# A hybrid decoder layer whose order is made by a cost model: new figures in the model, and a 64-row block transposed by VectorE instead of TensorE

## The chip, the cores and the metric

The kernel runs on one core of a Trainium2 chip. The metric is the time of one execution on the device in microseconds (us); lower is better. A core has five engines that run side by side, each with its own queue that it works through in order: TensorE (PE; its weight loads are listed apart as PEld), VectorE (DVE), ScalarE (ACT), GpSimd (POOL) and SyncE (SP), which issues most of the DMAs. An engine waits for another one on semaphores.

## The reference: what is computed

One decoder layer on 2048 tokens of width 1024, in float32. A mixer of two parallel head groups and an MLP, each followed by a layer norm:

```python
o = chunk_gated_delta_rule(q, k, v, g, beta)      # 8 heads of 128, chunks of tokens
m = memory_attention(mq, mem_k, mem_v)            # 4 heads over 256 memory rows
mix = concatenate([rms_norm(o) * silu(z), m]) @ w_out
x = layer_norm(ALPHA * x + mix)
x = layer_norm(ALPHA * x + square(relu(x @ w1)) @ w2)
```

The projection of x gives q, k, v (each through a causal convolution of four taps and a SiLU), the gate z, the decay and beta, and the memory query. Inside a chunk the delta rule solves a triangular system. The kernel does it with chunks of 128 tokens, by inverting a unit lower triangular matrix:

```python
lower = where(strict, (k_beta @ k.T) * decay, 0.0)
a_mat = eye + lower
u = triangular_solve(a_mat, v_beta, lower=True, unit_diagonal=True)
```

## The kernel before

**Tiling.** The tokens go in four blocks of 512 (`NB` blocks of `TB`). Each block passes three stages: the DeltaNet stage (projections, convolution, inversion, state scan, memory attention), the output projection with the first norm, and the MLP with the second. The MLP's second matrix product is done in seven products of sums of quarter matrices instead of eight (`ff_seven`, a Strassen-like scheme listed in `SEVEN`, L987); the sums of weight quarters are made in block 0 by `keep_sums` and put into a DRAM scratch called `tsc`, from which all blocks read them.

**Precision.** A large product is made of three fp32r matmuls, high x high, high x low and low x high (`mm3`). So each weight tile is loaded into `wraw` (three buffers), split by ACT (the high part) and DVE (the low part) into `whl` (four buffers), and read by PE. Tiles named `aq`, `ak`, `av`, `az`, `amq`, `ao`, `af` are PSUM results of such products, 24 matmuls of 512 columns each for a projection.

**DeltaNet by heads.** In step t of a block, `dense` projects head t, `gdn_a` prepares head t-1 (its matrix `dl`, the inversion, `ptv`), and `gdn_b` runs the state scan of head t-2 over four chunks of 128 tokens: pc and po on PE, R on DVE, vt on ACT, state on DVE. All are recorded one after the other but overlap in time.

**The inversion** (`invert`, L732). Four 128x128 matrices of a head are inverted together. 16-row blocks are solved on DVE in 15 steps (tiles `Xc` and `Bc`). Then the blocks are merged three times, to 32, 64 and 128 rows. Each merge has a product `pq` on PE, a copy to `Q` on ACT, a product `pp` on PE, and a subtraction or a multiply by -1 on DVE. `Y3` holds the transposed inverse; `X32` and `X64` hold the untransposed blocks that `pp` needs as weights. For the last merge, `X64` is made from `Y3` by four 64x64 transposes on PE into `px` (L799 to L801) and a copy by DVE (L802). Tiles pq, px and pp of one head parity share one PSUM bank (`ga0` or `ga1`).

**What sets the order.** The program isn't issued as it is written. `Recorder` (L135) keeps every operation, `cost` (L184) gives it a duration, and `issue` (L220) runs a list schedule: at each step the engine that is free first takes, of its operations that are ready, the one that was recorded first. The order so found is then issued to the engines' queues. All of these instructions therefore carry the line L320 in the profile, and are told apart by their tiles' names. For PE the model has two figures per matmul: `load` for the weights, which may overlap the matmul before, and `last` for the streaming. An operation that another engine releases counts as ready after a latency (`LAT`, `LAT_FROM`, L33 and L34) and a margin of 30 ns (`MARGIN`). A DMA takes 1700 ns and its bytes at a modelled rate, one after the other.

**Memory.** `raw` (two buffers in pool `tp`) holds a projection before the convolution; `keep_sums` uses it too. Behind `tp` lies a pool `pad` with one tile of 112 words that nothing reads (L372, L373), and behind that the pools `sp` and `sm`.

Of the kernel before, what the change touches and what calls it, by code (L numbers as in the profile page):

```python
# [8 lines left out]
F32 = mybir.dt.float32  # L9
# [5 lines left out]
P = 128  # L15
TB = 512
NC = TB // P
# [17 lines left out]
MARGIN = 30  # L35


def _prod(v):
    r = 1
    for a in v:  # L40
        r *= a
    return r
# [92 lines left out]
class Recorder:  # L135
# [47 lines left out]
    @staticmethod  # L183
    def cost(o, name, wr, rd, args, kw):  # L184
        e = o.eng
        shapes = [r.shape for r in wr] + [r.shape for r in rd]
        n = max([_prod(s[1:]) for s in shapes] or [1])
        if e == "PE":
            rhs = kw.get("rhs", args[2])
            mo, n = _prod(args[1].shape[1:]), _prod(rhs.shape[1:])  # L190
            f32 = name == "transpose" or isinstance(rhs, Ref) and rhs.buf.dtype == F32
            o.load = 0.8 * mo
            o.last = 2.4 + (0.8334 if f32 else 0.4167) * n
            if name == "transpose":
                return o.last
            if f32:
                return o.last + max(o.last, o.load)
            return o.last
        psum = any(r.buf.psum for r in rd + wr)
        if e == "SP":  # L200
            o.extra = 1700 + _prod(wr[0].shape if wr else rd[0].shape) * 4 / 250.0
            return 450
        scal = [v for v in args[2:] if isinstance(v, Ref)] if name.startswith("tensor_scalar") else []
        scal += [v for k, v in kw.items() if k in ("scalar", "scalar1", "scale", "bias") and not isinstance(v, (int, float))]
        if e == "ACT":
            n = _prod((wr[0]).shape[1:])
            return 52 + 0.833 * n + (0 if psum else 42) + 93 * len(scal) + ((305 if scal else 198) if "accum_out" in kw else 0)
        if e == "DVE":
            fast = not psum and name in ("tensor_copy", "tensor_scalar_mul", "tensor_scalar_add", "tensor_scalar_max",
                                         "memset")  # L210
            return 68 + (0.52 if fast else 1.042) * n + 62 * len(scal) + (7 * n if name == "reciprocal" else 0)
        if name == "memset":
            return 40 + 0.83 * n
        if kw.get("op") == ALU.pow:
            return 300 + 165 * n
        if name == "tensor_copy":
            return 119 + 3.34 * n
        return 150 + 2.1 * n if name == "tensor_tensor" else 176 + 3.34 * n

    def issue(self):  # L220
# [49 lines left out]
        while True:  # L270
            while pending:
                place(pending.pop(0))
            best = None
            for e in engs:
                if avail[e]:
                    t = free[e]
                elif soon[e]:
                    t = max(free[e], soon[e][0][0])
                else:
                    continue  # L280
                if best is None or t < best[0]:
                    best = (t, e)
            if best is None:
                break
            t, e = best
            while soon[e] and soon[e][0][0] <= t:
                r, i, o = heapq.heappop(soon[e])
                heapq.heappush(avail[e], (o.prio, i, o))
            o = heapq.heappop(avail[e])[2]
            if e == "PE":  # L290
                t = max(t, fed + o.load)
                fed = t + o.dur - o.last
            o.start, o.end = t, t + o.dur
            free[e] = o.end
            if o.extra:
                dma[0] = max(o.end + 1700, dma[0]) + o.extra - 1700
                o.end = dma[0]
            out.append(o)
            for s in o.succ:
                lat = LAT.get((e, s.eng), LAT_FROM[e])  # L300
                if lat:
                    lat += MARGIN
                s.ready = max(s.ready, o.end + lat)
                s.npred -= 1
                if s.npred == 0:
                    pending.append(s)
            for b in o.bufs:
                b.users -= 1
                b.end = max(b.end, o.end)
                if b.users == 0:  # L310
                    heapq.heappush(slots[b.key], b.end + LAT_FROM[e] + MARGIN)
                    again(b.key)
# [24 lines left out]
def hybrid_layer(  # L337
# [24 lines left out]
    nc = tc.nc  # L362
# [6 lines left out]
    cst = ctx.enter_context(tc.tile_pool(name="cst", bufs=1))  # L369
    wp = ctx.enter_context(tc.tile_pool(name="wp", bufs=1))  # L370
    tp = ctx.enter_context(tc.tile_pool(name="tp", bufs=1))
    pad = ctx.enter_context(tc.tile_pool(name="pad", bufs=1))  # L372
    nc.vector.memset(pad.tile([P, 112], F32, name="shift"), 0.0)  # L373
    sp = ctx.enter_context(tc.tile_pool(name="sp", bufs=1))
    sm = ctx.enter_context(tc.tile_pool(name="sm", bufs=1))
    ps = ctx.enter_context(tc.tile_pool(name="ps", bufs=1, space=bass.MemoryType.PSUM))
# [296 lines left out]
    def dense(b, h, T, G, w0=None):  # L673
        res = {}
        for nm, o in (("q", QO), ("k", KO), ("v", VO), ("z", ZO)):
            w = w0 if w0 and nm == "q" else load_in(b, o // P + h)
            a = bank("a" + nm, "acc")
            project(a, w, T)
            c = slot("c" + nm, "d")
            th = slot("th", "th")  # L680
            if nm == "z":
                nc.scalar.activation(th, a, AF.Tanh, scale=0.5)
                nc.vector.scalar_tensor_tensor(out=c, in0=th, scalar=1.0, in1=a, op0=ALU.add, op1=ALU.mult)
            else:
                gi = o // P + h
                raw = rec.buf(tp, (P, TB + 3), F32, "raw", 2, "raw")
                nc.scalar.copy(out=raw[:, 3:], in_=a)
                nc.gpsimd.tensor_copy(raw[:, 0:3], halo[:, gi].part(gi))
                if b < NB - 1:
                    nc.gpsimd.tensor_copy(halo[:, gi].part(gi), raw[:, TB:TB + 3])  # L690
                nc.scalar.activation(c, a, AF.Copy, scale=cw[:, 72 + gi:73 + gi])
                for j in range(3):
                    nc.vector.scalar_tensor_tensor(out=c, in0=raw[:, j:j + TB], scalar=cw[:, j * 24 + gi:j * 24 + gi + 1],
                                                   in1=c, op0=ALU.mult, op1=ALU.add)
                nc.scalar.activation(th, c, AF.Tanh, scale=0.5)
                nc.vector.scalar_tensor_tensor(out=c, in0=th, scalar=1.0, in1=c, op0=ALU.add, op1=ALU.mult)
            res[nm] = c
            if nm in "qk":
                if "kq" not in res:
                    res["kq"] = [rec.buf(tp, (P, 2, TB), F32R, "kq%d" % u, 1, "kq") for u in range(2)]  # L700
                i = "kq".index(nm)
                split(c, res["kq"][0][:, i].part(i), res["kq"][1][:, i].part(i), KQE)
# [29 lines left out]
    def invert(L, par):  # L732
# [47 lines left out]
        nc.vector.transpose(Z.rearrange("p c f -> p (c f)"), ZT.rearrange("p c f -> p (c f)"))  # L780
        for p in range(2):
            nc.vector.tensor_copy(X32[32 * p:32 * p + 32, :, 32 * p:32 * p + 32], Z[64 * p:64 * p + 32])
        for r in quads:
            nc.scalar.copy(out=Y3[r, :, r], in_=ZT[r])
        pq = bank("pq", "ga%d" % par)[:64, :P].rearrange("p (c f) -> p c f", c=NC)
        for c in range(NC):
            nc.tensor.matmul(pq[:, c], L32[:, c], ZT[:, c], start=True, stop=True)
        nc.scalar.copy(out=Q[:64, :, :32], in_=pq)
        pp = bank("pp", "ga%d" % par)[:64, :P].rearrange("p (c f) -> p c f", c=NC)
        for c in range(NC):  # L790
            nc.tensor.matmul(pp[:, c], X32[:, c], Q[:, c, :32], start=True, stop=True)
        for p in range(2):
            nc.vector.tensor_scalar_mul(Y3[64 * p:64 * p + 32, :, 64 * p + 32:64 * p + 64],
                                        pp[32 * p:32 * p + 32], -1.0)

        pq = bank("pq", "ga%d" % par)[:64, :2 * P].rearrange("p (c f) -> p c f", c=NC)
        for c in range(NC):
            nc.tensor.matmul(pq[:, c], L[:, c, :64], Y3[:, c, 64:], start=True, stop=True)
        px = bank("px", "ga%d" % par)[:64, :2 * P].rearrange("p (c f) -> p c f", c=NC)  # L799
        for c in range(NC):  # L800
            nc.tensor.transpose(px[:, c], Y3[:64, c, :64], ident[:64, :64])  # L801
        nc.vector.tensor_copy(X64[:64], px)  # L802
        nc.scalar.copy(out=Q[:64], in_=pq)
        pp = bank("pp", "ga%d" % par)[:64, :2 * P].rearrange("p (c f) -> p c f", c=NC)
        for c in range(NC):
# [165 lines left out]
    def keep_sums(u, j):  # L971

        if j == 0:
            B = [t[:, n * TB:(n + 1) * TB].part(n) for t in (tok_tile("wq"), tok_tile("wq")) for n in range(2)]
        else:
            B = [rec.buf(tp, (P, TB + 3), F32, "raw", 2, "wq")[:, :TB] for _ in range(2)]
            kq = rec.buf(tp, (P, 2, TB), F32, "kq1", 1, "wq")
            B += [kq[:, n].part(n) for n in range(2)]
        for n in range(4):
# [11 lines left out]
    def ff_seven(b, ff1_tiles, relu2, add, norm2):  # L991
        Q = 2 * P
        for g in range(NS):
# [45 lines left out]
            if last:  # L1039
                gb = load_bcast(ln2_g, "l2g"), load_bcast(ln2_b, "l2b")  # L1040
            banks = {}
            for n, (xn, wn, bn, on, (th, nh)) in enumerate(SEVEN):
                if not on:
                    banks[bn] = [bank("af2", ("ga%d" % t) if bn == "A" else "pb") for t in range(2)]
                w = [None, None]
# [223 lines left out]
```

## Time and profile before

| what | us |
|---|---|
| median of three runs | 2998.03 |
| lowest and highest of them | 2996.6 and 2998.27 |
| the profiled execution | 2999.08 |
| its span, from the first to the last instruction | 2997.4 |

A block of 512 tokens takes some 734 us. The stages of the second block are the pattern for the third and the fourth: DeltaNet from 784 to 1108 us after the span's start, output projection to 1184, MLP to 1518. Block 0 has its DeltaNet stage from 0 to 350, with the memory's keys and values and the high and low parts of the input weights made beside it.

How to read the rows. A row of the timeline has the start, the duration, engine, line, operation, out<-in, the shape, a count of merged instructions and, in brackets, the idle time of the engine before it and what ended that. A group row has busy time and the mean in ns of one instruction, then idle time before the group. For a matmul, "64*64" is the size of the weight block. Matmuls are pipelined, so a matmul's own duration is longer than the distance from its start to the next one's start; the distance is what one matmul costs. An instruction that waits holds up all behind it in its engine's queue.

### The profile page before, as it was taken

The page shows a single profiled execution, that of the slowest core. Times are in us where ns is not written, and L with a number is a line of the kernel's source. Part 1 is how long each engine was busy: PE and PEld are TensorE (multiplying, and loading weights), DVE is VectorE, ACT ScalarE, POOL GpSimd, SP SyncE. Part 2 cuts the span into 40 slices and gives each one's busy share as a digit, 9 for nine tenths or more (in the row PEclk, how much of TensorE's full clock was granted, in tenths as well). Part 3 has the DMA queues.
Part 4 walks back from the last instruction along what each step waited for, and adds up shares of the span by engine and source line. Part 5 has one row for each costly group of instructions (what it writes and reads, how often), then busy time and mean ns, then how long its engine had stood idle before and what let it go on. Part 6 is the DMA issues. An engine that isn't in the chain of part 4 may idle for free.

```text
span 2997.4 us, 43880 instructions
## 1 busy us (share of the span) xinstructions
PE 2945.4 (98%) x15300; PEld 2428.1 (81%) x15300; DVE 2168.6 (72%) x5537; ACT 1520.3 (51%) x3582; POOL 332.4 (11%) x808
## 2 busy tenths in 40 slices
PE   7999999999999999999999999999999999999998
PEld 6888788888788878888878887888878888788886
DVE  6898977666777787655577887665667787675667
ACT  5676534544355562544445665344554556444443
POOL 1222100000112211000012221000001222000000
PEclk9999999999999999999999999999999999999999
DMA  6765566656733223444473332244446332324443
GB/s 231 253 218 180 196 209 224 200 183 192 268 142 132 106 89 102 145 137 133 151 268 130 121 119 92 87 152 144 145 159 250 126 134 96 99 88 146 143 147 134
DMA packets 127709, 469.85 MB, mean 157 GB/s; under 512 B 14464, under 2 KB 16896, under 8 KB 109056
## 3 DMA queue, kind: packets, MB, share of 16 engines
q1 hardware_dynamic: 126912, 467.00, 46.2%
q8 instruction: 120, 1.97, 0.3%
q14 instruction: 101, 0.83, 0.1%
q10 hardware_dynamic: 576, 0.06, 0.0%
HBM read 402.97 MB, written 64.03 MB: 156 GB/s over the span
## 4 chain that ended last, share of the span: by engine, by line
PE 88%; DVE 8%; ACT 2%; issue 1%; DMA 1%; POOL 0%; POOLq 0%; ACTq 0%; DVEq 0%; SPq 0%
PE af L320 42%; PE ao L320 8%; PE aq L320 6%; PE ak L320 5%; PE az L320 5%; PE av L320 4%; PE amq L320 3%; PE pc L320 3%; PE pp L320 2%; PE pq L320 2%; PE po L320 2%; PE pkq L320 1%; DVE y L320 1%; PE sps L320 1%; DVE ck L320 1%
## 5 line engine op out<-in xcount | busy, mean ns | idle before, releaser
L320 DVE TENSOR_TENSOR whl<-wraw,whl 128x1024 fp32r<-128x1024 f32 (+1 forms) x446 | 538.7, 1216 | 392.8 <-ACT whl L320 386.1
L320 PE MATMUL af<-Thi,whl 128*128 128x512 f32 (+1 forms) x2304 | 655.9, 369 | 6.9 <-DVE whl L320 4.0
L320 ACT CAST whl<-wraw 128x1024 fp32r<-128x1024 f32 (+1 forms) x446 | 466.1, 1045 | 381.8 <-PE af L320 169.0
L320 PEld LDWEIGHTS af<-Thi,whl 128*128 128x128 f32 x2304 | 421.7, 191 | 78.5 <-DVE whl L320 4.8
L320 PE MATMUL af<-whl,xh 128*128 128x512 f32 x1536 | 476.4, 391 | 3.6 <-DVE whl L320 3.6
L320 PE MATMUL af<-Tlo,whl 128*128 128x512 f32 (+1 forms) x1152 | 424.8, 369 | 0.0
L320 PE MATMUL af<-whl,xl 128*128 128x512 f32 x896 | 347.3, 390 | 0.0
L320 PEld LDWEIGHTS af<-whl,xh 128*128 128x128 f32 x1536 | 288.6, 188 | 68.6 <-DVE whl L320 6.7
L320 PE MATMUL ao<-whl,ch 128*128 128x512 f32 x768 | 249.4, 399 | 0.5 <-DVE y L320 0.5
L320 PEld LDWEIGHTS af<-Tlo,whl 128*128 128x128 f32 x1152 | 220.4, 191 | 34.8
L320 ACT ACTIVATE rl<-af 128x512 f32<-128x512 f32 x128 | 76.5, 598 | 271.0 <-PE af L320 269.0
L320 DVE SCALAR_TENSOR_TENSOR y<-y,af 128x512 f32<-128x512 f32 x224 | 151.3, 684 | 84.1 <-PE af L320 82.9
L320 PEld LDWEIGHTS af<-whl,xl 128*128 128x128 f32 x896 | 168.5, 188 | 35.5
L320 POOL TENSOR_SCALAR ve<-mv 128x1 f32<-128x1 f32 x34 | 23.3, 684 | 1528.8 <-DVE mv L320 1528.8
L320 PE MATMUL aq<-Thi,whl 128*128 128x512 f32 x512 | 181.6, 414 | 7.5 <-ACT Thi L320 7.5
L320 PE MATMUL av<-Thi,whl 128*128 128x512 f32 x512 | 173.0, 402 | 0.0
L320 PE MATMUL ak<-Thi,whl 128*128 128x512 f32 x512 | 172.9, 401 | 0.0
L320 PE MATMUL az<-Thi,whl 128*128 128x512 f32 x512 | 170.2, 400 | 0.0
L320 PEld LDWEIGHTS ao<-whl,ch 128*128 128x128 f32 x768 | 142.6, 188 | 27.0 <-DVE y L320 0.7
L320 PE MATMUL ao<-whl,cl 128*128 128x512 f32 x384 | 153.5, 400 | 0.0
L320 PEld LDWEIGHTS aq<-Thi,whl 128*128 128x128 f32 x512 | 94.3, 192 | 21.5 <-ACT Thi L320 7.5
L320 PEld LDWEIGHTS az<-Thi,whl 128*128 128x128 f32 x512 | 95.9, 190 | 18.8 <-DVE whl L320 0.5
(252 smaller groups left out, 5756.3 us busy)
## 6 DMA issues: line engine op xcount, KB each, us to landing
wraw<-in_w_ff_dram SPq DMA_DIRECT2D x224, 512.0 KB, 4.0
whl<-wsc SPq DMA_DIRECT2D x108, 1024.0 KB, 4.8
wraw<-tsc SPq DMA_DIRECT2D x128, 512.0 KB, 3.3
wsc<-whl SPq DMA_DIRECT2D x36, 1024.0 KB, 4.9
wraw<-in_w_out_dram SPq DMA_DIRECT2D x48, 512.0 KB, 4.1
wraw<-in_w_in_dram SPq DMA_DIRECT2D x35, 512.0 KB, 5.8
wq<-in_w_ff_dram SPq DMA_DIRECT2D x64, 256.0 KB, 4.3
tsc<-wq SPq DMA_DIRECT2D x64, 256.0 KB, 3.3
```

The lines of the kernel that those rows point to most:

```text
L320: o.fn(*[res(a) for a in o.args], **{k: res(v) for k, v in o.kw.items()})
```

## The change

Four things change in the planner's model: a weight load is modelled as 4 + 0.84 ns per column instead of 0.8 ns per column; an fp32r matmul streams for 13.4 + 0.4167 ns per column instead of 2.4 + 0.4167; a DMA runs at 300 GB/s instead of 250; and an operation on PE that another engine releases counts as ready a weight load later. In the inversion, the four transposes to `px` and their copy go. `X64` is put together from parts: its two diagonal 32-row blocks are copied by POOL from `Z`, and the block below the diagonal comes from a VectorE transpose of the 32-row product `pp`, in PSUM, into a free part of `Lq`, and a multiply by -1. In the first group of block 0, product `A12` is recorded as the second of the seven instead of the sixth. The `pad` pool goes and each of the two `raw` buffers grows by 56 words.

```diff
-            o.load = 0.8 * mo
-            o.last = 2.4 + (0.8334 if f32 else 0.4167) * n
+            o.load = 4 + 0.84 * mo
+            o.last = 2.4 + 0.8334 * n if f32 else 13.4 + 0.4167 * n
...
-            o.extra = 1700 + _prod(wr[0].shape if wr else rd[0].shape) * 4 / 250.0
+            o.extra = 1700 + _prod(wr[0].shape if wr else rd[0].shape) * 4 / 300.0
...
-                    lat += MARGIN
+                    lat += MARGIN + (s.load if s.eng == "PE" else 0)
...
-    pad = ctx.enter_context(tc.tile_pool(name="pad", bufs=1))
-    nc.vector.memset(pad.tile([P, 112], F32, name="shift"), 0.0)
...
-                raw = rec.buf(tp, (P, TB + 3), F32, "raw", 2, "raw")
-                nc.scalar.copy(out=raw[:, 3:], in_=a)
+                raw = rec.buf(tp, (P, TB + 3 + 56), F32, "raw", 2, "raw")
+                nc.scalar.copy(out=raw[:, 3:TB + 3], in_=a)
...
             nc.vector.tensor_copy(X32[32 * p:32 * p + 32, :, 32 * p:32 * p + 32], Z[64 * p:64 * p + 32])
+            nc.gpsimd.tensor_copy(X64[32 * p:32 * p + 32, :, 32 * p:32 * p + 32], Z[32 * p:32 * p + 32])
...
-        pp = bank("pp", "ga%d" % par)[:64, :P].rearrange("p (c f) -> p c f", c=NC)
+        p32 = bank("pp", "ga%d" % par)
+        pp = p32[:64, :P].rearrange("p (c f) -> p c f", c=NC)
         for c in range(NC):
             nc.tensor.matmul(pp[:, c], X32[:, c], Q[:, c, :32], start=True, stop=True)
+        t32 = Lq[:32].rearrange("p f c -> p (f c)")
+        nc.vector.transpose(t32, p32[:32, :P])
         for p in range(2):
             nc.vector.tensor_scalar_mul(Y3[64 * p:64 * p + 32, :, 64 * p + 32:64 * p + 64],
                                         pp[32 * p:32 * p + 32], -1.0)
+        nc.vector.tensor_scalar_mul(X64[32:64, :, :32], t32.rearrange("p (c f) -> p c f", c=NC), -1.0)
...
-        px = bank("px", "ga%d" % par)[:64, :2 * P].rearrange("p (c f) -> p c f", c=NC)
-        for c in range(NC):
-            nc.tensor.transpose(px[:, c], Y3[:64, c, :64], ident[:64, :64])
-        nc.vector.tensor_copy(X64[:64], px)
...
-            B = [rec.buf(tp, (P, TB + 3), F32, "raw", 2, "wq")[:, :TB] for _ in range(2)]
+            B = [rec.buf(tp, (P, TB + 3 + 56), F32, "raw", 2, "wq")[:, :TB] for _ in range(2)]
...
-            for n, (xn, wn, bn, on, (th, nh)) in enumerate(SEVEN):
+            order = [0, 5, 1, 2, 3, 4, 6] if b == 0 and g == 0 else range(7)
+            for n, (xn, wn, bn, on, (th, nh)) in enumerate(SEVEN[i] for i in order):
```

## The prediction

> **What bounds the kernel now.** I read the page first: engine shares, clock, chain.
>
> ```profile
> span 2997.4 us, 43880 instructions
> ...
> PE 2945.4 (98%) x15300; PEld 2428.1 (81%) x15300; DVE 2168.6 (72%) x5537; ACT 1520.3 (51%) x3582; POOL 332.4 (11%) x808
> ...
> PE 88%; DVE 8%; ACT 2%; issue 1%; DMA 1%; POOL 0%; POOLq 0%; ACTq 0%; DVEq 0%; SPq 0%
> ```
>
> TensorE (PE) is busy 98% of the span, and 88% of the chain that ended last is its own instructions. Only 2997.4 - 2945.4 = 52 us are idle. Where they lie is shown by the busy time per stage; the columns are PE, weight loads, DVE, ACT, POOL, then the granted clock (near 1 throughout), the DMA share and GB/s.
>
> ```profile
> 0.00:80.00 80.00, 64.18 (x317) 51.46 (x318) 55.70 (x115) 43.79 (x99) 15.43 (x49) 0.96 0.69 240
> 80.00:350.00 270.00, 269.67 (x1594) 221.56 (x1593) 242.07 (x860) 177.36 (x535) 65.26 (x162) 1.00 0.60 210
> 784.00:1108.00 324.00, 320.31 (x1859) 262.32 (x1857) 255.80 (x964) 181.20 (x602) 67.95 (x185) 1.00 0.40 143
> 1184.00:1518.00 334.00, 331.72 (x1548) 276.36 (x1547) 210.01 (x302) 162.10 (x225) 5.15 (x7) 0.99 0.47 149
> 2652.00:2997.00 345.00, 332.08 (x1551) 278.36 (x1549) 219.16 (x314) 157.42 (x217) 7.38 (x11) 0.98 0.43 139
> ```
>
> The start leaves PE idle for 15.8 us and the last stage, with the closing layer norms, for 12.9. A DeltaNet stage (784 to 1108, and its two repeats) leaves 3.7, an MLP stage 2.3. So about 52 - 28.7 = 23 us of idle time lie where a better order could fill them. The rest must come from PE doing less. A PE that counts as busy may still stand behind a weight load or a change of shape, so I then looked at starts in the timeline rather than at busy time.
>
> **The change, part by part. The transposes.** Each of the 32 inversions sends four 64x64 transposes (px) to PE. The first fence is the chain's price of dense and of 128x128 fp32 work, the second the timeline around one px group.
>
> ```profile
> 832.01 5.45 PE az L320 x24
> ...
> 842.71 0.44 PE ptq L320 x4
> ```
>
> ```profile
> 943.31 0.37 ACT L320 COPY Q<-pq 64x256 f32<-64x256 f32 x1 [2.86 <-PE pq L320]
> ...
> 943.72 0.39 PE L320 MATMUL aq<-Thi,whl 128*128 128x512 f32 x1
> 944.03 0.25 PEld L320 LDWEIGHTS px<-ident,Y 64*64 64x64 f32 x4 [0.36 <-ACT Q L320]
> 944.04 0.41 PE L320 MATMUL px<-ident,Y 64*64 64x64 f32 x4
> ...
> 944.38 0.19 PEld L320 LDWEIGHTS ak<-Thi,whl 128*128 128x128 f32 x1
> 944.38 0.50 PE L320 MATMUL ak<-Thi,whl 128*128 128x512 f32 x1
> ...
> 944.71 0.39 PE L320 MATMUL ak<-Tlo,whl 128*128 128x512 f32 x1
> ```
>
> A dense matmul takes 5.45 / 24 = 0.227 us. From the aq matmul at 943.72 to the second ak at 944.71 are 0.99 us; without px they would hold two dense matmuls, 0.45. One group therefore costs 0.54 us, not the 0.34 from 944.04 to 944.38: PE loses about 0.09 before px and 0.11 after it, where ak's first weights load at the same moment as the matmul is shown to start. The profile puts the first loss on ACT's copy of Q, but that copy ended at 943.68, 0.35 us before the load: not a late operand. If it were, pp, which needs the same Q, would inherit 32 x 0.09 = 2.9 us. I take it to go.
>
> The Trainium skill, in "TensorEngine Tiling (Array Packing)", section Tiling Modes (Key Properties), says that "Changing tiling mode (not just tile) drains the TensorE"; a 64x64 block between 128x128 ones changes it twice. By that rule both losses go with px; by the profile's own releaser the sum is 2.9 us smaller. The trace agrees with the rule: the stop stands there with Q long done.
>
> 32 x 0.54 = 17.3 us. Six groups are split, two in each of the last three token blocks; the first and the last:
>
> ```profile
> 891.32 0.36 PE L320 MATMUL px<-ident,Y 64*64 64x64 f32 x3
> 891.61 0.49 PE L320 MATMUL pc<-vt,kd 128*128 128x128 f32 x2
> 891.93 0.39 PE L320 MATMUL po<-vt,at 128*128 128x128 f32 x2
> 892.25 0.24 PE L320 MATMUL px<-ident,Y 64*64 64x64 f32 x1
> 892.42 0.73 PE L320 MATMUL av<-Thi,whl 128*128 128x512 f32 x2
> ```
>
> ```profile
> 2432.35 0.36 PE L320 MATMUL px<-ident,Y 64*64 64x64 f32 x3
> ...
> 2433.27 0.24 PE L320 MATMUL px<-ident,Y 64*64 64x64 f32 x1
> ```
>
> Of the 1.10 us from 891.32 to 892.42, pc and po need about 0.44 (four at 0.44 / 4 = 0.11, as the ptq row has it); with 0.09 before and 0.11 after, px costs 0.86, 0.32 more than an unsplit group. 6 x 0.32 = 1.9, together **19.2 us of PE**. A second of PE is a second of span only where PE carries the chain, 88% by the page: 16.9 us. Bounds: nothing (rival C) to 19.2.
>
> **What replaces them.** On DVE one copy X<-px goes, a transpose of 32x128 from PSUM and a multiply into X64 come; on POOL two copies.
>
> ```profile
> L320 DVE TENSOR_SCALAR Y<-pp 32x128 f32<-32x128 f32 x64 | 18.0, 281 | 9.8 <-PE pp L320 8.7
> ...
> L320 DVE COPY X<-Z 32x128 f32<-32x128 f32 x64 | 14.2, 221 | 0.9
> L320 DVE COPY X<-px 64x256 f32<-64x256 f32 x32 | 13.3, 416 | 14.8 <-PE px L320 14.4
> ...
> L320 DVE STREAM_TRANSPOSE ZT<-Z 128x128 f32<-128x128 f32 x32 | 9.9, 309 | 0.4
> ```
>
> ```profile
> L320 POOL COPY L<-dl 32x128 f32<-32x128 f32 x64 | 31.2, 487 | 24.7 <-PE pq L320 14.9 <-DVE Bc L320 7.5
> ```
>
> A transpose out of PSUM is not in the trace; between the 221 ns of an SBUF copy of that size and the 416 of the PSUM copy I take the 309 of the SBUF transpose, the only transpose there is. DVE then does 309 + 221 - 416 = 114 ns more per inversion, 3.6 us in all. The cover is PE: DVE has 242 of 270 us busy in its fullest DeltaNet stage; uncovered, it costs those 3.6. The transpose also waits for pp on PE, as the two Y multiplies behind it do already, and pushes them and the matmul pq that reads Y by 0.3 us; but the px wait, its 0.34 on PE and the 0.42 of X<-px leave the same inversion, so its latency shrinks. The POOL copies add 64 x 0.487 = 31 us to an engine at 11%, between Z and the last pp, with two PE groups of slack; behind them wait only copies of the next head. All this: nothing, at worst 4 us.
>
> **The order of the seven products.** In the first group of block 0, A12 moves from sixth to second, ahead of S3, whose weights must come back from DRAM scratch (tsc).
>
> ```profile
> 513.89 0.51 PE L320 MATMUL af<-whl,xh 128*128 128x512 f32 x1 [0.29 <-DVE whl L320]
> ...
> 521.09 0.50 PE L320 MATMUL af<-whl,xh 128*128 128x512 f32 x1 [1.47 <-DVE whl L320]
> ```
>
> These stalls, 1.8 us idle, and the stretched weight loads before them are what 5 us of other work can cover: -2.0, bounds -3 and 0.
>
> **The model.** It issues nothing itself; it changes the order in which each engine's queue is filled. A matmul of 512 columns is now modelled at 13.4 + 213.3 = 226.7 ns, as traced above, instead of 215.7. Any PE operation released by another engine counts as ready a weight load later (4 + 0.84 x 128 = 111 ns), so another matmul goes first if one is ready. The weight loads of the state scan show what that can recover:
>
> ```profile
> PEld pc L320 <- ACT vt L320: 4.8, 17, 0.5
> PEld pc L320 <- DVE state L320: 4.4, 12, 0.5
> ...
> PEld pc L320 <- DVE R L320: 2.3, 8, 0.5
> ```
>
> That is 11.5 us. Against it, a chain on DVE now has 5% fewer dense matmuls beside it, so the PE operation at its end is queued earlier. Break-even is 111 ns / 5% = 2.2 us of chain: the scan's steps are shorter, the 15-step solve is longer. I take a quarter of 11.5, **-3 us**; bounds -20 (most of the 23 idle) and +35 (rival D). SP's 300 instead of 250 GB/s shortens a 512 KB load from 3.8 to 3.45 us in the model; on the page it is 4.0:
>
> ```profile
> wraw<-in_w_ff_dram SPq DMA_DIRECT2D x224, 512.0 KB, 4.0
> ```
>
> The buffers bound how early a load can start, so I take nothing. The removed memset and the wider raw (2 x 56 words for 112) leave the pools behind at their addresses: nothing.
>
> Sum against the profiled execution (2999.08 us, of which 1.7 lie outside the span): 2999.1 - 16.9 - 2.0 - 3 = 2977.2. That execution was 1.05 above the median 2998.03, so I forecast **2976 us**; its own range is 2963 to 2988.
>
> **The rivals. B: the waits go too.** If the model's order fills most of the 23 us idle, 20 instead of 3, the time is 2976 - 17 = 2959. For: the idle is scattered and dense matmuls usually stand ready. Against: much of it hangs on weights at a stage's start, where nothing else is ready:
>
> ```profile
> PE af L320 <- DVE whl L320: 7.6, 10, 1.5
> ```
>
> **C: the freed time becomes waiting.** The DeltaNet stages end some waits on DVE (the 8% of the chain); if the heads' DVE work sets their pace, PE idles 0.54 us longer per inversion. Then only the reordering stays: 2998 - 2 = 2996. For: DVE at 242 of 270. Against: in that stage PE has 0.3 us idle.
>
> **D, slower: the long chain comes too late.** Place: the first pq of an inversion, behind the solve on DVE.
>
> ```profile
> 1591.38 0.25 DVE L320 TENSOR_SCALAR Lc<-Lq,half 128x64 f32<-128x64 f32 x1
> ...
> 1600.51 0.31 DVE L320 STREAM_TRANSPOSE ZT<-Z 128x128 f32<-128x128 f32 x1
> ```
>
> ```profile
> 1600.98 0.91 PE L320 MATMUL pq<-ZT,LB 128*112 128x16 f32 x8
> ```
>
> ```profile
> 1669.70 0.93 PE L320 MATMUL pq<-ZT,LB 128*112 128x16 f32 x8 [0.34 <-DVE Bc L320]
> ```
>
> The solve takes 9.4 us here; pq is queued 5% of that, 0.47 us, earlier, less 0.1. PE's queue is in order, so all dense matmuls behind pq wait, and those feed the next head. At 0.37 us x 32 = 12 us the gain is halved; from 22 / 32 = 0.69 us per inversion it is gone, and at 1.1 us (35) the time is 2976 + 35 = 3011. For: pq waits already. Against: one of two heads shown waits 0.34 us, the other's pq at 1600.98 none.
>
> **How the numbers follow.** A measurement of this kernel tells 0.2%, 6 us, from no change. Forecast 0.56 and B 0.14 are faster: 0.70. C 0.15 is within 0.2%. D 0.15 is slower. The range reaches from B's 2959, less 4 for a DVE cover that holds everywhere, to the upper end of C: 2955 to 3000. It leaves out D and a little below B.
>
> **What would show it.** Right: PE with 128 fewer instructions, no px, dense matmuls still 0.227 us apart, PE's idle not above 52 us, the DeltaNet stages 3 to 5 us shorter each. The order step is right if af's waits between 500 and 530 us are gone. Wrong: longer waits at pq or ptk (D), DVE on the chain well over 8% (C), or new stalls in the MLP stages, which I expect unchanged.

## The result, and the profile after

The changed kernel takes 2967.24 us (median; the runs lie between 2965.98 and 2976.73) against 2998.15 us for the kernel before on the same chip: 30.9 us less, a ratio of 0.9905 with a 95% interval of 0.9884 to 0.9926. Taken a second time on another chip (`g1_after_again`, below) it gave 2969.71 us against 2997.13, 0.9908. The forecast was 2976 us. Runs of one kernel differ with the granted clock of TensorE: the kernel before takes 2996.0 to 2997.6 us at 0.997 and 2998.7 to 3000.0 at 0.995 (one run of `d2_72cols_all`, at 0.778, took 3472 us and is left out).

The page of the kernel after, span, engines and chain:

```profile
span 2966.1 us, 43768 instructions
...
PE 2922.6 (99%) x15172; PEld 2410.1 (81%) x15172; DVE 2178.7 (73%) x5568; ACT 1518.2 (51%) x3582; POOL 342.1 (12%) x872
...
PE 81%; DVE 8%; ACT 7%; DMA 2%; issue 2%; POOL 1%; ACTq 0%; POOLq 0%; DVEq 0%
```

The profiled execution took 2967.86 us, 31.2 less than that of before. PE has 128 instructions fewer and 22.8 us less busy time (2945.4 to 2922.6); its idle time fell from 52 to 43.5 us, by 8.5. So three quarters came from a PE that does less or does it closer together, a quarter from waits. DVE stayed at 8% of the chain; ACT went from 2% to 7%.

Busy time per stage of the kernel after, in the columns of the table of before:

```profile
0.00:80.00 80.00, 67.44 (x344) 55.04 (x345) 62.77 (x141) 47.12 (x103) 20.82 (x56) 0.98 0.84 294
80.00:350.00 270.00, 266.71 (x1580) 218.67 (x1579) 242.73 (x866) 176.82 (x550) 61.55 (x168) 1.00 0.57 195
784.00:1108.00 324.00, 322.50 (x1883) 264.70 (x1882) 257.52 (x969) 188.90 (x623) 68.87 (x195) 1.00 0.38 133
1184.00:1518.00 334.00, 333.34 (x1497) 274.06 (x1496) 218.58 (x334) 162.01 (x228) 8.71 (x15) 1.00 0.52 165
```

The windows are the old ones, while the work has moved forward under them, so they show density and not the length of a stage: PE is idle for 12.6 us at the start (15.8 before), 3.3 in block 0's DeltaNet stage (0.3 before), 1.5 instead of 3.7 in the second block's, 0.7 instead of 2.3 in its MLP.

Lengths need an anchor that moves with the work. I take the first matmul of the output projection (`ao`) in each block, from the timeline; the distance from one to the next is a whole block. All in us, of the profiled executions, with the parts that were run alone for later use:

| from, to | before | inverse alone (a2) | model alone (a3) | after | after with the old times (f2) |
|---|---|---|---|---|---|
| start, block 0 | 350.0 | 353.0 | 355.9 | 350.8 | 343.7 |
| block 0, block 1 | 747.0 | 740.4 | 734.5 | 728.3 | 727.3 |
| block 1, block 2 | 734.1 | 728.0 | 732.2 | 730.5 | 723.8 |
| block 2, block 3 | 734.2 | 729.6 | 735.0 | 728.4 | 724.0 |
| block 3, end | 432.1 | 430.1 | 430.6 | 428.1 | 431.5 |

More than half of the gain, 18.7 us, lies in one period, from block 0 to block 1, which holds the sums of the weight quarters; the steady blocks give 3.6 and 5.8.

### The profile page after: what moved, and what is told of

Read it like the earlier page. It is cut to its first block, busy times and chain, and to the rows that moved or that the text cites. A ratio compares the mean times of both kernels' runs of the same rounds, so it can differ in the third digit from the quotient of the medians.

```text
span 2966.1 us, 43768 instructions
## 1 busy us (share of the span) xinstructions
PE 2922.6 (99%) x15172; PEld 2410.1 (81%) x15172; DVE 2178.7 (73%) x5568; ACT 1518.2 (51%) x3582; POOL 342.1 (12%) x872
## 4 chain that ended last, share of the span: by engine, by line
PE 81%; DVE 8%; ACT 7%; DMA 2%; issue 2%; POOL 1%; ACTq 0%; POOLq 0%; DVEq 0%
PE af L320 40%; PE ao L320 6%; PE az L320 5%; PE av L320 5%; PE ak L320 4%; PE aq L320 4%; PE amq L320 3%; PE pc L320 3%; DVE y L320 2%; PE pp L320 2%; PE pq L320 2%; PE po L320 2%; PE pkq L320 1%; DVE whl L320 1%; PE sps L320 1%
## 5 line engine op out<-in xcount | busy, mean ns | idle before, releaser
L320 PE MATMUL az<-Thi,whl 128*128 128x512 f32 x512 | 177.3, 406 | 1.1 <-DVE whl L320 1.1
L320 POOL MEMSET Y<- 128x512 f32 x32 | 16.8, 525 | 1037.9 <-PE af L320 921.0
```

Source lines behind the costliest of these rows:

```text
L320: o.fn(*[res(a) for a in o.args], **{k: res(v) for k, v in o.kw.items()})
```

## The experiments

Each kernel is compared with the kernel before on the same chip; where two of one batch are compared with each other, the text says so. Four kernels take the change apart, one more takes its buffers alone, four undo one part of it in the changed kernel, two test what 64-column blocks cost on PE, and one repeats it.

**The px groups left out, order frozen.** The planner still plans them and nothing else moves; they and their copies are only not issued, so that the output lacks what the last merge makes of `X64`.

```diff
+                if any(isinstance(a, Ref) and a.buf.name == "px" for a in o.args):
+                    continue
```

> The kernel before, planned as before, but the px transposes and the copy X<-px are left out when the order is issued, so that X64 stays zero and the last merge of the inverse is missing from the output. Nothing else moves. If a px group costs TensorE its shape changes too (0.54 us, 0.86 where split), 19.2 us of TensorE go and 16.9 of the span: 2981 us (2978 to 2984). If the loss ahead of px belongs to Q and is inherited by pp, 2984 to 2987. If only the 0.34 us from the first px to the next start goes, 2987. If the freed time becomes waiting, 2996 or more.

Measured: 2978.71 against 2997.72 us, 0.994 (0.9924 to 0.9957), **-19.0 us** (13 to 23 by the interval). The sum for PE alone was 19.2; with the factor of 0.88 it was 16.9, which the interval holds too. The page of this kernel, span and engines:

```profile
span 2975.9 us, 43598 instructions
...
PE 2922.9 (98%) x15172; PEld 2413.7 (81%) x15172; DVE 2157.5 (72%) x5505; ACT 1520.9 (51%) x3582; POOL 334.1 (11%) x808
```

PE's idle time is 53.0 us, 1 more than before, and its busy time is 22.5 less: no freed time became waiting (rival C). Nor did pp inherit a wait for Q, which would have added 2.9 us: the steps from the start of the matmul ahead to the start of the last merge's pp sum to 10.0 us before and to 9.9 here, over the 32 inversions. That PE is named for 88% of the chain does not make 0.88 the worth of a second taken from it: PE is busy 98% of the span, its idle time hardly grew, and the middle of the interval is at 19.0.

**The inverse alone.** Before, with the diff's edit of the inversion and nothing else.

> The kernel before with the change of the inverse alone (DVE transpose, POOL copies, no px), the old model. The px theory with a DVE that is hidden: 2981 us, give or take 5 for the new order. If DVE's 3.6 us and the POOL copies are not hidden: 2985 or more. If nearly all of the 31 us came from the inverse: 2970.

Measured: 2981.42 us, 0.9949 (0.9934 to 0.9964), **-16.3 us**. In the same batch the transposes gave 19.0. The 2.7 us between the two lie inside both intervals, and at the same granted clock, 0.996, the two kernels run alike (2979.83 and 2979.96 us here, 2979.03 and 2980.43 without px). So what replaces the transposes, with the new plan that it makes, gives back nothing to some 3 us, of the 4 that I had as the worst.

**The model alone.** Before, with the three edits of the model.

> The kernel before with the three figures of the model alone, px kept. If the 31 us are px (17) and order (2) with the rest from the model, 12: 2986 us (2982 to 2990). By the size of the forecast, 3: 2995. If the model does nothing: 2998. If the long chains come too late: over 3000.

Measured: 2991.78 us, 0.998 (0.997 to 0.9989), **-5.9 us**; nine runs spread from 2987.19 to 2997.15. By the table above the gain is not spread over the scans, where I put it: block 0 to block 1 is 12.5 us shorter, the first stage 5.9 longer, and the two steady periods change by -1.9 and +0.8.

**The order of the seven products alone.**

```diff
-            for n, (xn, wn, bn, on, (th, nh)) in enumerate(SEVEN):
+            order = [0, 5, 1, 2, 3, 4, 6] if b == 0 and g == 0 else range(7)
+            for n, (xn, wn, bn, on, (th, nh)) in enumerate(SEVEN[i] for i in order):
```

> The kernel before with A12 as the second product in the first group of block 0, alone. The stalls of af between 510 and 530 us (1.8 us idle, 2.5 us with the weight loads) go: 2996 us (2995 to 2996.5). Rival: they return at the next product that reads tsc, 2998.

Measured: 2997.86 against 2997.72 us, 1.0 (0.999 to 1.0009): **nothing**. The timeline of this kernel, PE, two rows between 515 and 523 us:

```profile
515.13 0.49 PE L320 MATMUL af<-whl,xh 128*128 128x512 f32 x1 [1.45 <-DVE whl L320]
...
522.38 0.49 PE L320 MATMUL af<-whl,xh 128*128 128x512 f32 x1 [1.45 <-DVE whl L320]
```

The interval, 3 us either way, would hold a gain of 2.0, but the stalls that it was to come from didn't go; they moved by a microsecond and together are 2.9 us, against 1.8 before.

**The old order in the changed kernel.** The change with `enumerate(SEVEN)` as before.

> The changed kernel with the seven products of the first group back in their old order. Alone on the kernel before, the order gave nothing (2997.9 against 2997.7). If it gives nothing here either: 2967 us. If it works only with the new model, which fills block 0's MLP stage 2.9 us better than the two parts do in their own runs: 2970.

Measured: 2968.47 us, 0.9899 (0.9882 to 0.9915), as the whole change. Between 490 and 780 us no wait of PE is listed at all for this kernel; with the new order there is one, of 0.2 us. So the waits of af that I gave to the order were taken away by another part. The model alone leaves a single wait of af between 350 and 784 us, of 0.9 us.

**The buffers: in the change as they were, and alone.** In e2 the pool `pad` and raw's old width return to the changed kernel; b4 is the kernel before with pad gone and raw wider. The order of every engine is kept, in e2 that of the change and in b4 that of before; only addresses and the memset differ. Of e2:

```diff
...
-                raw = rec.buf(tp, (P, TB + 3 + 56), F32, "raw", 2, "raw")
+                raw = rec.buf(tp, (P, TB + 3), F32, "raw", 2, "raw")
...
```

> The changed kernel with the pad pool and the narrow raw buffers back. The planner sees the same shapes, so the order is the same and only addresses differ. The forecast was nothing: 2967 us. In the profile, matmuls that stream hq take 389 ns after and 394 before and in the three runs with old buffers: if that is the address, 256 x 5 ns = 1.3 us, 2968.5.

> The kernel before with the wide raw buffers and without the pad pool, the same order on every engine. If addresses explain the 4 to 6 us between the changed kernel and its copy with old buffers: 2992 to 2994, with hq matmuls 389 instead of 394 ns. If only the hq stream is an address effect (1.3 us) and the rest of that difference was the granted clock (0.997 against 0.998): 2996 to 2997.

Measured: e2 2973.95 us, 0.9919 (0.9904 to 0.9934), 5.5 us slower than e1 of the same batch (which differs from the change by the order of the products, worth nothing); b4 2994.1 against 2997.13 us, 0.9989 (0.9981 to 0.9998), **-3.0 us**. What I had put at nothing is some 3 to 5 us (four runs each of e2, 2971.1 to 2978.2, and of e1, 2967.5 to 2973.0). One of the seven-product groups shows part of it, here of e2 and of b4 (before has 80.1 us and 394 ns, as e2 has):

```profile
L320 PE MATMUL af<-whl,hq 128*128 128x512 f32 x256 | 80.1, 394 | 0.0
```

```profile
L320 PE MATMUL af<-whl,hq 128*128 128x512 f32 x256 | 78.8, 389 | 0.0
```

The same 256 matmuls, in the same places, take 5 ns less each: 1.3 us. (hq is their weight operand, and whl is what streams.) The rest is at their neighbours: from start to start, af's matmuls from xh take 1.1 us less in b4 than before and those from xl 0.8 us less (391 to 390 and 390 to 389 ns each in the rows). With hq that is 3.2 us, the whole of the 3.0; between e1 and e2 the same three groups differ by 3.3 us. The 2 us that e2 loses beyond them have no row.

**The model without the load behind a wait.** The change, with one of the model's edits undone.

```diff
-                    lat += MARGIN + (s.load if s.eng == "PE" else 0)
+                    lat += MARGIN
```

> The changed kernel without the weight load behind each wait; traced times and 300 GB/s stay. If this term carries the model's gain (6 us alone, some 14 on top of the inverse): 2973 to 2981 us. If the traced times carry it: 2967. If the term costs time: under 2965.

Measured: 2983.42 us, 0.9949 (0.9934 to 0.9964), **15.0 us slower** than e1 of the same batch; by the two runs of each at a granted clock of 0.997, 11.6 us. The weight loads' waits show where; first of f1, then of the kernel after (total, times, longest):

```profile
PEld pc L320 <- DVE state L320: 10.1, 38, 0.7
PEld pc L320 <- DVE R L320: 7.9, 32, 0.5
...
PEld pc L320 <- ACT vt L320: 4.2, 19, 0.4
```

```profile
PEld pc L320 <- DVE state L320: 3.2, 6, 0.8
...
PEld pc L320 <- DVE R L320: 2.3, 8, 0.4
...
PEld pc L320 <- ACT vt L320: 1.1, 5, 0.5
```

With the term the scan's three waits go from 22.2 us in 89 cases to 6.6 in 19. This is the effect that I argued for, 15.6 us of it, but against traced times without the term. Against before, whose same three rows are the 11.5 us of the prediction, it is 4.9 us, and in the model alone, where they are 9.6, it is 1.9.

**The model with the old times.** The change, with the old durations of PE's loads and matmuls; the load behind a wait and 300 GB/s stay.

```diff
-            o.load = 4 + 0.84 * mo
-            o.last = 2.4 + 0.8334 * n if f32 else 13.4 + 0.4167 * n
+            o.load = 0.8 * mo
+            o.last = 2.4 + (0.8334 if f32 else 0.4167) * n
```

> The changed kernel with the old matmul and weight load times in the model, but with the weight load behind each wait and 300 GB/s. If that term alone carries the model's gain: 2967 us, 3 either way. If the traced times matter too: 2972 or more. If the 5% slower matmul in the model queues long chains too early, as the slower rival of the forecast had it: under 2964.

Measured: **2953.24 us**, 0.9854 (0.9841 to 0.9868), 16.5 us faster than the change repeated in the same batch and the fastest kernel of all; at the same granted clock the gap is 13 to 15 us (2952.05 to 2953.41 against 2965.98 us at 0.998, 2955.19 against 2969.56 and 2969.86 at 0.997). By the table of periods it is faster in nearly every stretch. Its page and PE's waits, then PE's waits of the kernel after (idle in total, times, longest; the wait at the start, 7.7 and 7.2 us, is left out):

```profile
span 2950.3 us, 43795 instructions
...
PE 2913.0 (99%) x15172; PEld 2420.0 (82%) x15172; DVE 2169.4 (74%) x5568; ACT 1518.6 (51%) x3582; POOL 350.9 (12%) x872
```

```profile
PE af L320 <- DVE whl L320: 3.9, 4, 1.0
PE pkq L320 <- ACT jq L320: 2.7, 1, 2.7
PE af L320 <- ACT whl L320: 2.6, 4, 0.7
...
PE ptq L320 <- ACT kd L320: 1.4, 1, 1.4
```

```profile
PE pp L320 <- ACT Q L320: 4.2, 9, 0.6
PE pkq L320 <- ACT jq L320: 3.7, 4, 2.7
PE af L320 <- DVE whl L320: 3.4, 6, 0.7
PE af L320 <- DVE Tlo L320: 1.9, 3, 0.6
PE ptq L320 <- ACT kd L320: 1.8, 2, 1.5
```

The wait of pp for Q is the one that the old times hardly have (0.2 us in f2). PE's idle time is 37.3 us against 43.5. Idle time alone is too small a measure, so I counted, in both traces, how much longer than usual each step from one matmul's start to the next is (usual is the median for the shape; what a step starts early is taken off the next). Steps that are 0.4 to 1 us too long: 34 with 20.9 us in the kernel after, 10 with 6.6 us in f2. Stalls above 1 us go the other way, 6.8 against 11.7. Together that is 9.4 of the 15.8 us between these two spans; steps less than 0.4 us too long make up the rest. Of the 20.9 us, 5.6 stand at the first merge's pp behind Q (0.5 in f2), 2.7 at the first pq and 2.6 at pkq (none in f2).

**One product with 72 columns.** PE's 64-column weight blocks are the suspect for the 0.09 and 0.11 us beside each px group. Four products of each inversion have such blocks still. Here the last merge's `pq` takes 72 columns of `L` in place of 64, the planner's cost unchanged; eight rows of the result are not read.

```diff
...
-            nc.tensor.matmul(pq[:, c], L[:, c, :64], Y3[:, c, 64:], start=True, stop=True)
+            nc.tensor.matmul(p72[:, c], L[:, c, :72], Y3[:, c, 64:], start=True, stop=True)
...
```

> The changed kernel, planned in exactly the same order, but the product pq of the last merge has weight blocks of 72 columns instead of 64 (the eight extra result rows are not read). If the loss before and after a 64-column block is the change of shape, as taken for px, a group loses about 0.10 us before and 0.09 after, less 8 x 7 ns of longer loads: 32 x 0.13 = 4 us less, 2963 us. If the loss is a late operand or the wait itself: 2967 or 1 to 2 us more.

Measured: 2963.83 us, 0.9885 (0.987 to 0.9899), 4.6 us less than e1 of the same batch. The same place in the timeline, PE, of the kernel after and of d1:

```profile
1593.61 0.38 PE L320 MATMUL pc<-R,Y 128*128 128x128 f32 x2
1593.92 0.68 PE L320 MATMUL pq<-Y,dl 128*64 128x64 f32 x8
1594.53 0.50 PE L320 MATMUL ak<-Thi,whl 128*128 128x512 f32 x1
1594.86 0.39 PE L320 MATMUL ak<-Tlo,whl 128*128 128x512 f32 x1
```

```profile
1592.93 0.38 PE L321 MATMUL pc<-R,Y 128*128 128x128 f32 x2
1593.14 0.67 PE L321 MATMUL pq<-Y,dl 128*72 128x64 f32 x8
1593.63 0.48 PE L321 MATMUL ak<-Thi,whl 128*128 128x512 f32 x1
1593.95 0.39 PE L321 MATMUL ak<-Tlo,whl 128*128 128x512 f32 x1
```

From pc to pq go 0.31 us with 64 columns and 0.21 with 72; from pq to the next ak 0.61 and 0.49. A wider block, which has more to load, is 0.22 us cheaper, with no operand earlier or later. In this one group the blocks of 64 columns cost 0.10 us on the way in and 0.12 on the way out. Times 32 groups that would be 7 us, but this is one of the dearer ones: over all groups of the two traces the way in is 1.9 us shorter and the rest, from pq's start to the next matmul's, 3.3. These 5.2 us agree with the 4.6. In 19 of 33 places (one group is split) the way in is 0.08 to 0.10 us shorter, in the other 14 less than 0.04 or not at all.

**All four products with 72 columns.** `L32`, `X32` and `X64` become 72 wide. To make room `raw` is narrowed by 48 words, so the pools behind keep their addresses, but what lies before them, the four `whl` buffers among it, moves by 384 bytes. The order of every engine is that of the change.

```diff
-        for n, f in (("XB", P), ("LB", P), ("L32", 64), ("X32", 64), ("X64", 64), ("Q", 64)):
+        for n, f in (("XB", P), ("LB", P), ("L32", 72), ("X32", 72), ("X64", 72), ("Q", 64)):
...
-                raw = rec.buf(tp, (P, TB + 3 + 56), F32, "raw", 2, "raw")
+                raw = rec.buf(tp, (P, TB + 3 + 8), F32, "raw", 2, "raw")
...
```

> The changed kernel in the same order, with weight blocks of 72 columns instead of 64 in all four 64-column products of an inversion (three buffers widened, raw narrowed by as much so that what lies behind keeps its address). One product gave 3.4 us, 0.11 us per group. If the shape change costs the same at each: 4 x 3.4 = 14 us less, 2954 us. If the stages' waits on DVE and ACT take part of it: 2957 to 2961.

Measured: 2972.45 us, 0.9914 (0.9899 to 0.993): no gain, 2.7 us more than the change repeated in the same batch. By the count of steps, those that are 0.06 to 0.13 us too long fell from 58.8 to 32.2 us, so the shape changes are off PE's small groups. The time came back in the large ones; groups of the kernel after, then of d2:

```profile
L320 PE MATMUL af<-whl,xh 128*128 128x512 f32 x1536 | 474.8, 390 | 1.3 <-DVE whl L320 0.7 <-ACT whl L320 0.2
L320 PE MATMUL af<-whl,xl 128*128 128x512 f32 x896 | 346.0, 389 | 0.0
```

```profile
L321 PE MATMUL af<-whl,xh 128*128 128x512 f32 x1536 | 482.1, 395 | 0.2 <-DVE whl L321 0.2
L321 PE MATMUL af<-whl,xl 128*128 128x512 f32 x896 | 350.7, 394 | 0.0
```

Each matmul takes 5 ns more: 7.3 and 4.7 us, with 2.9 for `ao` from ch, 1.3 for `ao` from cl and 1.4 for `af` from hq by the same view, 17.6 us; from start to start, which is the cost, the same matmuls take 19.6 us more. The four products gain less than the count says: from the start of the matmul ahead to the start of the one behind they are 14.9 us shorter, since the last merge's pq now waits for Y. PE's wait there, of the kernel after, then of d2:

```profile
PE pq L320 <- DVE Y L320: 0.4, 2, 0.2
```

```profile
PE pq L321 <- DVE Y L321: 2.7, 8, 0.5
```

19.6 less 14.9 are 4.7 us; the profiled execution of d2 is 4.6 us longer than that of the change. The slower matmuls are those that stream whl. Those that stream Thi and Tlo, with whl as their weights, step as before (af from Thi every 226.6 ns, in d2 226.7). That the move of the buffers does it is an inference: order and work are the same, and addresses are what else differs. A kernel with the move alone was not run.

**The change once more**, as the partner of this batch.

> The changed kernel itself, so that the others of this group can be held against it on one chip: 2967 us (2965 to 2969).

Measured: 2969.71 against 2997.13 us, 0.9908 (0.9895 to 0.9922), -27.4 us.

## Why the prediction was right, and where it was wrong

The direction and the largest term were right; the time, 2967 against 2976 us, came out lower because the model's term was sized too small, the buffers' was set at nothing, and all together gave more than the parts, while the order's term, which I counted, isn't there. Part by part, each alone against before:

| part | forecast | alone |
|---|---|---|
| transposes and what replaces them | -16.9 | -16.3 |
| order of the seven products | -2.0 | +0.1 |
| model | -3 | -5.9 |
| raw and pad | 0 | -3.0 |
| sum | -21.9 | -25.1 |

All together gave -30.9, and -27.4 the second time. The 2 to 6 us over the sum may be interplay of one part's plan with another's; they are no larger than the intervals of the parts, so this isn't shown.

**The transposes: right.** The price from starts, 0.54 us for a group that shows 0.34, gave 19.2, measured 19.0. The stop ahead of px was read as a change of shape and not as a late Q; a1 bears it out, since the steps onto pp did not grow, and d1 shows the two losses at another group by size, 0.10 and 0.12 us beside 0.09 and 0.11. The Trainium skill's rule, in "TensorEngine Tiling (Array Packing)", Tiling Modes (Key Properties), that a change of the tiling mode drains TensorE, agrees with these runs for 64 columns between 128; it states no time for it. Another narrow block shows no such loss. In the kernel before, `aab` has weights of 32 columns and streams 512, and its steps in and out are those of full blocks:

```profile
2238.25 0.39 PE L320 MATMUL af<-whl,xl 128*128 128x512 f32 x1
2238.48 0.39 PE L320 MATMUL aab<-Thi,abw 128*32 128x512 f32 x1
...
2239.17 0.39 PE L320 MATMUL aab<-Tlo,abw 128*32 128x512 f32 x1
2239.39 0.61 PE L320 MATMUL af<-whl,xh 128*128 128x512 f32 x2
```

From af to aab are 0.23 us, from aab to af 0.22. So that the 64-column blocks of the inversion cost these times is shown; that it is because of the drain is not. The factor 0.88, the share of the chain read as an exchange rate, has nothing in the runs for it: 19.0 us came of 19.2, though the interval of 13 to 23 can't exclude 16.9.

**What replaces them: right, within its bounds.** Rows of VectorE, then of GpSimd, of the kernel after:

```profile
L320 DVE STREAM_TRANSPOSE Lq<-pp 32x128 f32<-32x128 f32 x32 | 9.7, 302 | 18.2 <-PE pp L320 18.1
...
L320 DVE TENSOR_SCALAR X<-Lq 32x128 f32<-32x128 f32 x32 | 7.3, 229 | 0.6
```

```profile
L320 POOL COPY X<-Z 32x128 f32<-32x128 f32 x64 | 24.1, 377 | 101.5 <-DVE Z L320 87.0 <-PE pq L320 11.9 <-DVE Xc L320 0.8
```

The transpose from PSUM is 302 ns (309 estimated), with the multiply 302 + 229 - 416 = 115 ns more per inversion (114 forecast). The POOL copies are 377 ns each, not 487. The 0 to 3 us that came back in a2 lie inside the 0 to 4 that I gave for a cover that is gone; which instruction would cost them isn't shown.

**The order of the products: wrong.** The step "-2.0, bounds -3 and 0" landed on its end. I argued that 5 us of other work ahead of S3 covers its weights; a4 shows the same stalls a microsecond later, and e1 shows them gone without that edit. The sign that I had named for this step, af's waits between 500 and 530 us gone, did appear, and would have borne out a wrong step: a sign that two steps can both produce tells neither apart.

**The model: right in sign, wrong in place and size.** "A quarter of 11.5 us" of the scan's waits was to go. Alone the model gave -5.9, all of it in the period from block 0 to block 1, and nothing in the steady blocks. Inside it are two halves that nearly cancel: the load behind a wait is worth 12 to 15 us within the change (f1), the traced times cost 13 to 16 (f2). The prediction had neither size, so that their net lies near its -3 is luck. Rival D priced the second at 35 us and more, as the whole model's result, and placed it at pq behind the solve on DVE. Little of it happened there: the idle time before pq<-ZT,LB is 1.7 us after, 1.2 in f2 and was 1.9 before, and steps more than 0.13 us too long take 3.9 us there after and 2.8 in f2. More stands at pp behind ACT's Q (6.9 against 2.6 us by the same count), the end of a short chain, which my break-even of 2.2 us had put among those that gain. That wait takes both figures together: PE's idle time for Q is 4.2 us after, but 0.2 in f2, 1.4 in f1 and 1.6 before. The change with neither figure was not run; an estimate from a2 and b4 is 2978 us (2997.1 - 16.3 - 3.0), by which the load term alone would gain some 25 us and the traced times alone would cost some 5. So a cost in D's direction is shown, by f2, and its mechanism is not; why figures nearer to the trace make a worse plan beside the load term stays open. One reading is that ACT's chains to Q and jq are planned too short, but no run changed ACT's costs.

**300 GB/s at nothing** was not run alone. f2 keeps it and is the fastest, so it does no great harm there; more can't be said.

**The pools' addresses at nothing: wrong**, by 3 to 5 us; I had reasoned that the pools behind `tp` stay where they are, and overlooked the tiles in `tp` itself: raw's second buffer moves by 224 bytes and what follows it by up to 448.

**Rival B** asked for 20 us of idle time to go; 8.5 went. **Rival C** is excluded by a1.

**The signs.** 128 fewer PE instructions, no px, PE's idle at 43.5 us, DVE at 8% of the chain: as forecast. DeltaNet stages 3 to 5 us shorter: by whole blocks 3.6 and 5.8 (5.7 and 1.4 in the repeat, whose second holds a stretch from 2400 to 2500 us at a granted clock of 0.95), about as forecast, though both halves of the model are in it. MLP stages unchanged: this can't be read as I put it, since the new order moves 14 of the next block's first aq matmuls (3.2 us) from ahead of the MLP's last matmul to behind it, and makes any MLP look shorter. In block 0 the MLP did gain: between 350 and 784 us af waited 4.9 us for whl before and 0.8 after.

## What to carry to other kernels

Price a small matmul group from the start of its last full-size neighbour to the start of the next one: here a group of 0.34 us cost 0.54, and making another one's block wider, 72 columns for 64, made it cheaper. When several figures of a planner change in one edit, run each alone within the change: one of these cost 13 to 16 us and another gained 12 to 15, together they looked like a small gain, and the version without the traced times takes 2953 us. And compare stages by an anchor that moves with the work, since a new order carries matmuls across the border of a fixed window.

## What the runs showed of the hardware that was not expected

The streaming of 512-column matmuls depends on something besides shape and order: 389 or 394 ns for `af` from hq with the old and the new buffers, 389 to 390 or 394 to 395 for `af` from xl and xh with `whl` moved by 384 bytes. The steps from start to start differ alike, 227 or 232 ns. Over 1536 matmuls the 5 ns are 7.3 us, more than most parts of this change. In the second case only the matmuls that stream `whl` got slower. Which addresses are the good ones no run here shows.

A group with fp32 weight blocks of 64 columns between blocks of 128 cost 0.10 us on entry and 0.12 on leaving; at 72 columns both were gone (0.31 to 0.21 us, and 0.61 to 0.49). A block of 32 columns that streams 512 columns of fp32r cost neither.
